# First branch's gates ahead of the second branch's operands, LayerNorm and RG-LRU in one pool, step sizes beside attention, PSUM handed over by bank

## The chip, the core and the metric

The kernel runs on one NeuronCore of a Trainium2 chip. The metric is the device time of one launch in microseconds (us), the median of several runs. All matrix products are float32 values split in two parts of a narrower float32 format, so that one product is three matmuls (high by high, high by low, low by high).

## What is computed

One layer of a streaming encoder for 1024 prompt frames and 64 sample frames (T = 1088 columns), 1024 channels, four branches:

```python
h = rms_norm(x, p['norm_pre']); proj = h @ p['w_in']          # 80 chunks of 128 columns, and 8 columns ssd_dt
u_a = rg_lru(causal_dwconv(lru_x)) * silu(lru_g)              # a_t = exp(-8 r softplus(-lam)), h_t = a_t h_{t-1} + ...
u_b = rms_norm(ssd_scan(...) * silu(ssd_z))                   # dt = softplus(ssd_dt + dt_bias), chunks of frames
u_c = silu(layer_norm(causal_dwconv(glu))) * silu(cf_g)
u_d = stick_breaking(q, k, v) * silu(sb_g)
mixed = sum over b of sigmoid(merge_b) * (u_b @ w_down[b])
y = x + rms_norm(mixed @ w_out)
```

## The kernel before, in words

Activations lie channel-major in `hh` and `hl`, 128 x 8 x 1088 each, the high and low part of the normalised input. A chunk of the input projection is 24 matmuls for each of three column pieces (384, 384, 320). The program runs in stages that TensorE works through in written order (L193: its order is the program's; the other engines' queues and the queue of SyncE, which issues all transfers, are ordered by a planner that goes by program order, with head starts such as W_PRIO for weight splits and C_PRIO for evacuations).

1. **Head**: normalise and transpose the input.
2. **Attention**: 68 units of scores, stick-breaking and output; between two units `feed.step` puts pieces of the other projections (L532: a quota that reaches 18 pieces per group of 17 units; in the last of the four groups 15 pieces are there). Constants for the SSD branch (`wdr`, `wd2`, `dtb_t`, `a_t`, `dsk`) stand behind this stage in the program.
3. **Spill stage** (L574 to L660): four chunks of the gate of branch C, in 12 pieces, each evacuated by ScalarE into `t` and stored; between them the sums and differences of the quarters of `hh` and `hl` (`g11`, `g12`, `g22`, `g21`: eight sums of 128 x 1088 on GpSimd at L601, the differences on VectorE) and their splits into `Th` and `Tl`; the product for the step sizes (L619, 48 matmuls), its transposes (L625), the softplus (`spd`), `adt`, and the two cumulative products at L641.
4. **Pair stage** (L663 to L1073): 20 pairs of chunks (gates of A, z of B, merge gates), each by a seven-product scheme (`ORDER`); after each of the 140 products a generator `chains()` is advanced by one step. It runs LayerNorm of branch C (`layer_norm`, 27 steps), RG-LRU (`lru`, a pool of its own on the right side of SBUF, three steps of waiting, then eight rounds of four steps) and SSD (`ssd`, three steps of waiting behind its first loads, then nine chunks). PSUM is a new pool here, `bank` x6 and `pg2` x2.
5. **Down stage** (L1079 on): for branch order 3, 0, 2, 1 and eight blocks of 128 rows each, a product into PSUM (`pj3` x6), multiplied by the gate `sga` (loaded by L1118, sigmoid at L1119) into `m`. `Operand` (L1082) loads a branch's `u` over dead parts of `hh` and `hl`. PSUM is a third pool.

A LayerNorm quarter q: `load`, mean product (L772), square, fold, three steps, variance product (L779), `lnr`, scale, SiLU, gate, split into `lnh` and `lnl`, stores (L793, L794), three steps. An RG-LRU round (c, j): load of `lg_t`, products for the two gates in two halves with a step between them, next round's `load`, Exp and Tanh (L852, L853), Sqrt, scan (L860), times `lg_t`, split into `uah` (which takes the slot of `ga`) and `ual` (which takes the slot of `lg_t`), stores, three steps.

A pool that is opened with `reuse_waits="tile"` makes each tile wait for what lay at its own addresses; without it, every tile of the new pool waits for the whole old pool.

Of the kernel before, what the change touches and what calls it, by code (L numbers as in the profile page):

```python
# [8 lines left out]
FT = mybir.dt.float32  # L9
# [36 lines left out]
def encoder_step(ctx, tc, x, prm, win, wdt, wdn, wout, lwa, lwx, ckT, cv_, ssd0, npre, npost, dtb, alog, dskip,  # L46
# [10 lines left out]
    ps = ps1.enter_context(tc.tile_pool(name="ps", bufs=1, space=PSUM))  # L57
# [452 lines left out]

    feed.add(cf_sig(0), cf_glu(0), k_chunk(0), q_chunk(0), g_chunk(0))
# [9 lines left out]
    for m, u in enumerate(units):  # L521
        c, k = divmod(m, NU)
        if k == 0:
            if c < 3:
                feed.add(cf_sig(c + 1), v_chunk(c + 1) if c else extra.pop(0), extra.pop(0), g_chunk(c + 1), cf_glu(c + 1), extra.pop(0))
            else:
                feed.add(*extra)
            fed = 0
# [3 lines left out]
        want = min(18, 18 * (k + 1) // (NU - 1))  # L532
# [19 lines left out]
        else:  # L552
# [3 lines left out]
            u.output(None)  # L556
    p1.close()
    p2.close()

    wdr = const.tile([128, 8, 8], FT, name="wdr")  # L560
    dma(wdr, wdt)
    wd2 = const.tile([128, 8, 16], FR, name="wd2")
    S.activation(wd2[:, :, 0:8], wdr, AF.Copy)
    V.tensor_sub(wd2[:, :, 8:16], wdr, wd2[:, :, 0:8].bitcast(FT))
    dtb_t = const.tile([128, 8], FT, name="dtb_t")
    dma(dtb_t, ap(dtb, 0, [[0, 128], [1, 8]]))
    a_t = const.tile([128, 8], FT, name="a_t")
    dma(a_t, ap(alog, 0, [[0, 128], [1, 8]]))
    S.activation(a_t, a_t, AF.Exp)
    dsk = const.tile([128, 4], FT, name="dsk")  # L570
    for h in range(2):
        dma(dsk[h * 64:h * 64 + 64, :], ap(dskip, h, [[0, 64], [2, 4]]))
# [15 lines left out]
    feed.add(*(spill(C_CG + c, cg_d[:, c]) for c in range(4)))  # L588
    feed.step(1)
# [6 lines left out]
    for k in (0, 2):  # L596
        g11, g12, g22 = (tmp.tile([128, 2, HT], FT, name=f"g{n}") for n in (11, 12, 22))
        g21 = tmp.tile([128, 2, HT], FT, name="g21", bufs=2)
        for g, kk, t in ((g11, k, tlo), (g12, k, thi), (g22, k + 4, thi), (g21, k + 4, tlo)):
            ks = slice(kk, kk + 2)  # L600
            G.tensor_tensor(g, hh[:, ks, t].bitcast(FT), hl[:, ks, t].bitcast(FT), op=OP.add)  # L601
# [8 lines left out]
        t4.append((kd, g21))  # L610
    feed.step(2)


    dtr = tmp.tile([16, T], FT, name="dtr")
    for i, (t0, n) in enumerate(SPL):
        p = pg()
        for k in range(8):
            for q, hx in enumerate((hh, hl)):
                PE.matmul(p[:16, :n], wd2[:, k, :], hx[:, k, t0:t0 + n], start=k == 0 and q == 0, stop=k == 7 and q == 1)  # L619
        S.activation(dtr[:, t0:t0 + n], p[:16, :n], AF.Copy)  # L620
    feed.step(3)
    pd = pg()
    for i in range(9):
        r = 128 if i < 8 else 64
        PE.transpose(pd[:r, i * 16:i * 16 + 16], dtr[:, i * 128:i * 128 + r], ident[:16, :16])  # L625
    pd3 = pd[:, :144].rearrange("p (i c) -> p i c", c=16)
    zb = tmp.tile([128, 9, 8], FT, name="zb", bufs=1)
    V.memset(zb, 0.0)
    for r, i0, i1 in ((128, 0, 8), (64, 8, 9)):
        V.tensor_tensor(zb[:r, i0:i1], pd3[:r, i0:i1, 0:8], dtb_t[:r, None, :].to_broadcast([r, i1 - i0, 8]), op=OP.add)  # L630
        V.tensor_tensor(zb[:r, i0:i1], pd3[:r, i0:i1, 8:16], zb[:r, i0:i1], op=OP.add)
    dt = dq.tile([128, 9, 8], FT, name="dt", bufs=1)
    V.tensor_copy(dt, softplus(tmp, zb, [9, 8], "spd"))
    adt = dq.tile([128, 9, 8], FT, name="adt", bufs=1)
    V.scalar_tensor_tensor(adt, dt, -1.0, a_t[:, None, :].to_broadcast([128, 9, 8]), op0=OP.mult, op1=OP.mult)
    V.memset(adt[64:128, 8, :], 0.0)
    feed.step(4)
    pa = pg()
    a2 = adt.rearrange("p i c -> p (i c)")
    PE.matmul(pa[:, 0:72], tri_le, a2, start=True, stop=True)  # L640
    PE.matmul(pa[:, 72:144], ones, a2, start=True, stop=True)  # L641
    acs = dq.tile([128, 2, 72], FT, name="acs", bufs=1)
    V.tensor_copy(acs, pa[:, :144].rearrange("p (a b) -> p a b", a=2))
    dtd = dq.tile([128, 9, 8], FT, name="dtd", bufs=1)
    d2 = dtd.rearrange("p i c -> p (i c)")
    V.tensor_sub(d2, acs[:, 1], acs[:, 0])
    S.activation(d2, d2, AF.Exp)
    S.activation(acs, acs, AF.Exp)
    eacs, etot = acs[:, 0], acs[:, 1]
    ah = dq.tile([128, 9, 8], FR, name="adh", bufs=1)  # L650
    al = dq.tile([128, 9, 8], FR, name="adl", bufs=1)
    split(ah, al, adt)
    V.tensor_tensor(dtd, dtd, dt, op=OP.mult)
# [9 lines left out]
    ps = ps2.enter_context(tc.tile_pool(name="ps2", bufs=1, space=PSUM))  # L663
# [84 lines left out]

    def layer_norm():
        lnp = ExitStack()  # L750
        ln = lnp.enter_context(tc.tile_pool(name="ln", bufs=1, side="right", reuse_waits="tile"))

# [13 lines left out]
        for q in range(4):  # L766
# [27 lines left out]
            dma(ul_d[2][:, :, t], gw.bitcast(FT))  # L794
            yield from wait(3)
        lnp.close()


    def lru():
        p4 = ExitStack()  # L800
        lp = p4.enter_context(tc.tile_pool(name="lru", bufs=1, side="right", reuse_waits="tile"))
        nl = lp.tile([128, 4], FT, name="nl")
        V.tensor_scalar(nl, P("lam", 0, 4), -1.0, None, op0=OP.mult)
        sp = softplus(lp, nl, [4], "spl")
        lm8 = lp.tile([128, 4], FT, name="lm8")
        lp4 = lp.tile([128, 4], FT, name="lp4")
        V.tensor_scalar(lm8, sp, -8.0, None, op0=OP.mult)
        V.tensor_scalar(lp4, sp, 4.0, None, op0=OP.mult)
        hfin = lp.tile([128, 2, 4], FT, name="hfin")
        raws = [lp.tile([128, 128], FT, name=f"bd{e}") for e in "ax"]  # L810
        for r_ in raws:
            G.memset(r_, 0.0)

        def load(c, j):
            t = slice(j * HT, j * HT + HT)
            if j == 0:
                self.bd = []
                for r_, src, e in zip(raws, (lwa, lwx), "ax"):
# [3 lines left out]
                    self.bd.append([lp.tile([128, 128], FR, name=f"bd{e}{f}") for f in "hl"])  # L822
                    split(*self.bd[-1], r_)
            xc = lp.tile([128, HT], FT, name="xl", bufs=2)
            dma(xc, xl_d[:, c, t])
            xh, xl = (lp.tile([128, HT], FR, name=f"xg{f}") for f in range(2))
            split(xh, xl, xc)
            return xc, xh, xl

        class self:  # L830
            pass
        todo = [(c, j) for c in range(4) for j in range(2)]
        nxt = load(0, 0)
        yield from wait(3)
        for m, (c, j) in enumerate(todo):
            t = slice(j * HT, j * HT + HT)
            xc, xh, xl = nxt
            g = lp.tile([128, HT], FT, name="lg_t")
# [3 lines left out]
            for t0 in (0, QT):  # L842
# [4 lines left out]
                if t0 == 0:  # L847
                    yield
# [410 lines left out]
```

## Time and profile before

| what | value |
|---|---|
| median of 3 runs | 1485.22 us (1483.89 to 1486.68) |
| profiled execution, its own time | 1485.71 us |
| span of its instructions | 1483.3 us |
| TensorE matmul busy | 1413.3 us (95%) |
| VectorE, ScalarE, GpSimd busy | 1067.1, 673.0, 263.0 us |
| mean granted TensorE clock | 0.986 |

A page of the profile gives busy times by engine, the span in 40 slices, and the costliest groups of instructions. Views of the trace give the waits by engine, single instructions in order of time with the idle time before them in brackets and what ended it, and sums over chosen stretches. TensorE's clock has two levels, 1.2 and 2.4 GHz, and the granted clock 0.50 and 1.00 of a stretch are these two.

### The profile page before, as it was taken

The page shows a single profiled execution, that of the slowest core. Times are in us where ns is not written, and L with a number is a line of the kernel's source. Part 1 is how long each engine was busy: PE and PEld are TensorE (multiplying, and loading weights), DVE is VectorE, ACT ScalarE, POOL GpSimd, SP SyncE. Part 2 cuts the span into 40 slices and gives each one's busy share as a digit, 9 for nine tenths or more (in the row PEclk, how much of TensorE's full clock was granted, in tenths as well). Part 3 has the DMA queues.
Part 4 walks back from the last instruction along what each step waited for, and adds up shares of the span by engine and source line. Part 5 has one row for each costly group of instructions (what it writes and reads, how often), then busy time and mean ns, then how long its engine had stood idle before and what let it go on. Part 6 is the DMA issues. An engine that isn't in the chain of part 4 may idle for free.

```text
span 1483.3 us, 25336 instructions
## 1 busy us (share of the span) xinstructions
PE 1413.3 (95%) x9857; PEld 1352.0 (91%) x9857; DVE 1067.1 (72%) x1628; ACT 673.0 (45%) x1225; POOL 263.0 (18%) x245
## 2 busy tenths in 40 slices
PE   6999999999999999899979989999999889999997
PEld 6899999999999998799979989999999789999885
DVE  6289889779879987847967775787877335669433
ACT  6324544544454365345769762443444242234211
POOL 0002221230221224613213231221211000000000
PEclk9999999999999999999989999999999989999999
DMA  6231212213212233134635444434343985643322
GB/s 210 75 87 54 82 47 83 87 55 95 84 56 79 66 102 107 41 125 142 212 135 175 152 138 139 131 108 154 120 133 96 329 333 170 244 155 109 105 86 71
DMA packets 113335, 184.43 MB, mean 124 GB/s; under 512 B 22080, under 2 KB 70080, under 8 KB 112704
## 3 DMA queue, kind: packets, MB, share of 16 engines
q1 hardware_dynamic: 113216, 182.82, 37.8%
q8 instruction: 77, 1.26, 0.4%
q14 instruction: 42, 0.34, 0.1%
HBM read 118.00 MB, written 60.59 MB: 120 GB/s over the span
## 4 chain that ended last, share of the span: by engine, by line
PE 40%; DVE 7%; ACT 4%; DMA 4%; issue 2%; SPq 0%; DVEq 0%; ACTq 0%
PE bank L721 16%; PE pj L109 7%; PE pj L110 7%; PE pj L111 7%; DVE w_lo L229 2%; DMA uh<-uoh 1%; DMA uh<-uah 1%; ACT w_hi L228 1%; DMA sga<-mgs 1%; PE pg L912 1%; DVE r L728 1%; PE pg L965 1%; ACT L852 1%; DVE lnx L787 0%; DVE yz L1005 0%
## 5 line engine op out<-in xcount | busy, mean ns | idle before, releaser
L110 PE MATMUL pj<-hl,w_hi 128*128 128x384 f32 (+4 forms) x1184 | 384.8, 325 | 1.6 <-DVE hl L225 1.6
L109 PE MATMUL pj<-hh,w_hi 128*128 128x384 f32 (+4 forms) x1088 | 354.7, 326 | 8.2 <-ACT t L584 5.5
L111 PE MATMUL pj<-hh,w_lo 128*128 128x384 f32 (+4 forms) x1088 | 352.3, 324 | 0.0
L110 PEld LDWEIGHTS pj<-hl,w_hi 128*128 128x128 f32 x1184 | 225.5, 190 | 3.5 <-DVE hl L225 2.5
L109 PEld LDWEIGHTS pj<-hh,w_hi 128*128 128x128 f32 x1088 | 206.5, 190 | 11.0 <-ACT t L584 5.6
L111 PEld LDWEIGHTS pj<-hh,w_lo 128*128 128x128 f32 x1088 | 206.2, 190 | 0.2
L721 PE MATMUL bank<-hh,w_hi 128*128 128x272 f32 x640 | 189.6, 296 | 1.8 <-ACT t L584 1.8
L721 PE MATMUL bank<-hh,w_lo 128*128 128x272 f32 x640 | 185.1, 289 | 0.0
L721 PE MATMUL bank<-hl,w_hi 128*128 128x272 f32 x640 | 185.1, 289 | 0.0
L243 DVE SCALAR_TENSOR_TENSOR cvo<-cbuf,p_t,cvo 128x1118 f32<-128x1118 f32 x120 | 165.5, 1380 | 1.8
L721 PE MATMUL bank<-Th,w_hi 128*128 128x272 f32 x480 | 143.1, 298 | 0.5 <-ACT r L725 0.5
L721 PE MATMUL bank<-Th,w_lo 128*128 128x272 f32 x480 | 139.8, 291 | 0.0
L721 PE MATMUL bank<-Tl,w_hi 128*128 128x272 f32 x480 | 139.6, 291 | 0.0
L721 PEld LDWEIGHTS bank<-hh,w_hi 128*128 128x128 f32 x640 | 121.4, 190 | 3.5 <-ACT t L584 2.0
L721 PEld LDWEIGHTS bank<-hl,w_hi 128*128 128x128 f32 x640 | 121.3, 189 | 0.6
L721 PEld LDWEIGHTS bank<-hh,w_lo 128*128 128x128 f32 x640 | 121.0, 189 | 0.0
L460 POOL TENSOR_SCALAR_AFFINE_SELECT fb<-fb 128x128 f32<-128x128 f32 (+1 forms) x72 | 38.6, 536 | 453.1 <-ACT fb L455 332.1
L463 DVE TENSOR_TENSOR_SCAN fb<-fb,ones 128x128 f32<-128x128 f32 (+8 forms) x68 | 90.0, 1324 | 27.5 <-POOL fb L460 27.4
L725 ACT ACTIVATE r<-bank 128x272 f32<-128x272 f32 x160 | 62.0, 391 | 91.1 <-PE bank L721 90.8
L102 DVE TENSOR_TENSOR w_lo<-w_raw,w_hi 128x1024 fp32r<-128x1024 f32 x56 | 70.9, 1266 | 44.4 <-ACT w_hi L101 43.9
L721 PEld LDWEIGHTS bank<-Th,w_hi 128*128 128x128 f32 x480 | 92.1, 192 | 2.6 <-issue 1.2
L101 ACT ACTIVATE w_hi<-w_raw 128x1024 fp32r<-128x1024 f32 x56 | 59.4, 1060 | 77.2 <-PE pj L110 69.1
(345 smaller groups left out, 2978.6 us busy)
## 6 DMA issues: line engine op xcount, KB each, us to landing
w_raw<-in_win_dram SPq DMA_DIRECT2D x80, 512.0 KB, 4.0
mgs<-r SPq DMA_DIRECT2D x64, 272.0 KB, 2.1
sga<-mgs SPq DMA_DIRECT2D x32, 544.0 KB, 4.2
w_raw<-in_wdn_dram SPq DMA_DIRECT2D x16, 512.0 KB, 4.6
xt<-in_x_dram SPq DMA_DIRECT2D x8, 512.0 KB, 9.4
xbc<-xc SPq DMA_DIRECT2D x8, 512.0 KB, 2.7
xb<-xbc SPq DMA_DIRECT2D x8, 512.0 KB, 5.6
w_raw<-in_wout_dram SPq DMA_DIRECT2D x8, 512.0 KB, 4.1
```

Of the source, the lines that this page charges most:

```text
L101: S.activation(hi, r3, AF.Copy)
L102: V.tensor_sub(lo, r3, hi.bitcast(FT))
L109: PE.matmul(out, ah, bh, start=first, stop=False)
L110: PE.matmul(out, ah, bl, start=False, stop=False)
L111: PE.matmul(out, al, bh, start=False, stop=last)
L228: S.activation(hi, src, AF.Copy)
L229: V.tensor_sub(lo, src, hi.bitcast(FT))
L243: V.scalar_tensor_tensor(out[:, :n], b[:, i:i + n], w[:, i:i + 1], out[:, :n], op0=OP.mult, op1=OP.add)
L460: G.affine_select(t_[s, 1024 - w:1024], t_[s, 1024 - w:1024], pattern=[[-1, w]], compare_op=OP.is_gt, fill=fill, base=0, channel_multiplier=1)
L463: V.tensor_tensor_scan(F[:, rev], F[:, rev], ones[:, 0:1].to_broadcast([128, n]), 1.0, OP.mult, OP.mult)
L721: PE.matmul(p, a_[:, k], b_[:, k, s], start=new and k == 0 and z == 0, stop=k == 3 and z == 2, skip_group_check=True)
L725: S.activation(R[to][:, s], p, self.last if j == 4 else AF.Copy)
```

## The change

It does eight things: all three PSUM pools are opened with `reuse_waits="tile"`; the constants of the SSD branch stand ahead of attention; the step-size product and its transposes become a generator fed in the last group of attention units, whose quota ends at 17; the softplus takes `lam` of RG-LRU along (76 columns) and stands at the head of the spill stage; the eight sums are VectorE's; the cumulative products stand between the two halves of the sums. LayerNorm's pool stays open for RG-LRU, whose tiles take LayerNorm's slots (`xg` that of `lnh`, `eg` that of `lng`, `rx` that of `lnx`, `uah`/`ual` that of `lns`, every second `xl` that of `lnq`); its first loads stand in LayerNorm's third and fourth quarter and its three waiting steps are gone; SSD waits five steps instead of three. In the down stage the eight gates of the first branch are loaded ahead of the second branch's operand, and their pool lies ahead of that of `m`.

```diff
-    ps = ps1.enter_context(tc.tile_pool(name="ps", bufs=1, space=PSUM))
+    ps = ps1.enter_context(tc.tile_pool(name="ps", bufs=1, space=PSUM, reuse_waits="tile"))
...
+    def step_sizes():
+        dtr = cp.tile([128, T], FT, name="dtr", tag="sb", bufs=1)
+        dts.append(dtr)
+        yield
+        for t0, n in SPL:
+            p = pg()
+            for k in range(8):
+                for q, hx in enumerate((hh, hl)):
+                    PE.matmul(p[:16, :n], wd2[:, k, :], hx[:, k, t0:t0 + n], start=k == 0 and q == 0,
+                              stop=k == 7 and q == 1)
+            S.activation(dtr[:16, t0:t0 + n], p[:16, :n], AF.Copy)
+            yield True
+        pd = dts[0] = pg()
...
-                feed.add(*extra)
+                feed.add(*extra, step_sizes())
...
-        want = min(18, 18 * (k + 1) // (NU - 1))
+        want = min(18 - (c == 3), (18 - (c == 3)) * (k + 1) // (NU - 1))
...
+    V.tensor_scalar(zl[:, 72:76], P("lam", 0, 4), -1.0, None, op0=OP.mult)
+    sp = softplus(tmp, zl, [76], "spd")
...
-            G.tensor_tensor(g, hh[:, ks, t].bitcast(FT), hl[:, ks, t].bitcast(FT), op=OP.add)
+            V.tensor_tensor(g, hh[:, ks, t].bitcast(FT), hl[:, ks, t].bitcast(FT), op=OP.add)
...
+        if k == 0:
+            feed.step(2)
+            pa = pg()
+            a2 = adt.rearrange("p i c -> p (i c)")
+            PE.matmul(pa[:, 0:72], tri_le, a2, start=True, stop=True)
...
-    ps = ps2.enter_context(tc.tile_pool(name="ps2", bufs=1, space=PSUM))
+    ps = ps2.enter_context(tc.tile_pool(name="ps2", bufs=1, space=PSUM, reuse_waits="tile"))
...
             if q < 3:
                 nxt = load(q + 1)
+            if q == 2:
+                lru.fetch(0, 0)
...
+            if q == 3:
+                lru.prepare(0, 0)
             yield from wait(3)
-        lnp.close()
...
+        def fetch(self, c, j):
             if j == 0:
...
+            xc = self.xc[c, j] = ln.tile([128, HT], FT, name="xl", tag=("xl", "lnq")[j])
+            dma(xc, xl_d[:, c, j * HT:j * HT + HT])
+
+        def prepare(self, c, j):
+            self.xg = ln.tile([128, 2, HT], FR, name="xg", tag="lnh")
+            split(self.xg[:, 0], self.xg[:, 1], self.xc[c, j])
+
+        def run(self):
...
+                eg = ln.tile([128, 2, HT], FT, name="eg", tag="lng")
+                ga, g = eg[:, 0], eg[:, 1]
+                dma(g, lg_d[:, c, t])
+                rx = ln.tile([128, 2, HT], FT, name="rx", tag="lnx", bufs=2)
+                gr, gx = rx[:, 0], rx[:, 1]
...
+                uh = ln.tile([128, HT], FR, name="uah", tag="lns", bufs=2)
+                ul = ln.tile([128, HT], FR, name="ual", tag="lns", bufs=2)
...
-        yield from wait(3)
+        yield from wait(5)
...
-    ps = ctx.enter_context(tc.tile_pool(name="ps3", bufs=1, space=PSUM))
+    ps = ctx.enter_context(tc.tile_pool(name="ps3", bufs=1, space=PSUM, reuse_waits="tile"))
...
-    us.append(Operand(order[1], [t_[:, k, thi] for t_ in (hh, hl) for k in (k0, k1)]))
-    mp = ctx.enter_context(tc.tile_pool(name="mp", bufs=1, reuse_waits="tile"))
-    mt = [mp.tile([128, T], FT, name=f"m{d}") for d in range(8)]
...
-    gates = [load_gate(order[0], d) for d in range(8)]
+    gates = [load_gate(order[0], d) for d in range(4)]
+    mp = ctx.enter_context(tc.tile_pool(name="mp", bufs=1, reuse_waits="tile"))
+    mt = [mp.tile([128, T], FT, name=f"m{d}") for d in range(8)]
+    gates += [load_gate(order[0], d) for d in range(4, 8)]
+    us.append(Operand(order[1], [t_[:, k, thi] for t_ in (hh, hl) for k in (k0, k1)]))
```

## Rows read from the trace of the kernel before

**Rows 1.** Waits of TensorE: instruction <- released by: us in total, times, longest us.
```profile
PE pj L109 <- DVE m L1150: 9.1, 1, 9.1
...
PE pg L109 <- ACT xg L228: 8.1, 1, 8.1
PE pj L109 <- ACT t L584: 5.5, 1, 5.5
PE pg L912 <- DVE lt L902: 4.5, 1, 4.5
...
PE pg L109 <- ACT gr L846: 2.7, 1, 2.7
PE pg L475 <- DVE beta L464: 2.3, 1, 2.3
...
PE bank L721 <- ACT t L584: 1.8, 1, 1.8
...
PE pj L109 <- ACT rs__12675 L1002: 1.4, 1, 1.4
```
**Rows 2.** Sums over stretches behind five waits: stretch, length, busy by engine, PEclk, DMA.
```profile
621.90:626.00 4.10, 4.10 (x13) 4.10 (x14) 4.10 (x4) 2.86 (x4) 0.00 (x0) 0.50 0.13 48
...
757.40:762.50 5.10, 4.93 (x20) 4.62 (x21) 0.70 (x1) 2.31 (x4) 0.00 (x0) 0.50 0.08 21
...
851.20:854.70 3.50, 3.50 (x17) 3.50 (x17) 3.47 (x9) 2.60 (x7) 1.00 (x1) 0.51 0.40 159
...
889.30:895.60 6.30, 6.30 (x22) 5.27 (x23) 3.15 (x6) 1.59 (x3) 0.00 (x0) 0.50 1.05 269
...
1190.40:1196.00 5.60, 5.60 (x25) 5.60 (x26) 2.10 (x6) 4.62 (x5) 0.00 (x0) 0.50 1.03 411
```
**Rows 3.** Sums over a stretch, of L619 alone: length, PE busy, PEld busy, PEclk, DMA.
```profile
595.00:604.00 9.00, 8.06 (x48) 4.53 (x48) 1.00 0.00 0
```
**Rows 4.** Spill stage: sum of L601 on POOL, three instructions, sum of tile spd.
```profile
583.87:648.20 64.33, 24.17 (x8) 0.95 0.23 76
...
605.93 3.63 DVE L607 TENSOR_TENSOR g<-g,g 128x1088 f32<-128x1088 f32 x1
...
622.73 1.28 DVE L607 TENSOR_TENSOR g<-g,g 128x1088 f32<-128x1088 f32 x1
...
620.32 1.11 ACT L228 ACTIVATE Th<-g 128x1088 fp32r<-128x1088 f32 x1 [9.30 <-DVE g L603]
...
627.50:634.50 7.00, 4.11 (x17) 0.26 (x1) 1.00 0.38 126
```
**Rows 5.** LayerNorm's last quarter to RG-LRU: instructions, one piece of the chain, landing of `lnh`.
```profile
730.48 0.72 PE L779 MATMUL pg<-lns,ones 128*128 128x272 f32 x2 [0.28 <-DVE lns L756]
...
731.20 15.07 PE bank L721 x120
...
743.77 1.11 ACT L228 ACTIVATE lnh<-lnx 128x1088 fp32r<-128x1088 f32 x1
...
DMA to landing us min/median/max: 3.3/3.6/4.3
...
756.68 0.66 ACT L228 ACTIVATE xg<-xl 128x544 fp32r<-128x544 f32 x1 [1.02 <-DMA xl<-xls]
```
**Rows 6.** RG-LRU: ScalarE's wait ahead of Exp, and a group in SyncE's queue.
```profile
842.75 1.28 ACT L852 ACT_TABLE_LOAD   x1 [2.81 <-DMA uh<-uah]
...
843.73 8.33 SPq L738 DMA_DIRECT2D mgs<-r  x3
```
**Rows 7.** Start of the down stage: SyncE's queue, ScalarE's wait, landing of the two weights.
```profile
1178.27 18.75 SPq L1118 DMA_DIRECT2D sga<-mgs  x10
1197.07 1.40 SPq L96 DMA_DIRECT2D w_raw<-in_wdn_dram  x1
...
1188.73 1.11 ACT L1119 ACTIVATE sga<-sga 128x1088 f32<-128x1088 f32 x1 [12.96 <-DMA sga<-mgs]
...
DMA to landing us min/median/max: 5.2/5.2/5.2
```

More of the change, by code (lines that the diff above doesn't have):

```diff
@@ L509, in output @@
             dma(ul_d[3][:, c, i * 128:i * 128 + m], ul[:, :m].bitcast(FT))
+    wdr = const.tile([128, 8, 8], FT, name="wdr")
+    dma(wdr, wdt)
+    wd2 = const.tile([128, 8, 16], FR, name="wd2")
+    S.activation(wd2[:, :, 0:8], wdr, AF.Copy)
+    V.tensor_sub(wd2[:, :, 8:16], wdr, wd2[:, :, 0:8].bitcast(FT))
+    dtb_t = const.tile([128, 8], FT, name="dtb_t")
+    dma(dtb_t, ap(dtb, 0, [[0, 128], [1, 8]]))
+    a_t = const.tile([128, 8], FT, name="a_t")
+    dma(a_t, ap(alog, 0, [[0, 128], [1, 8]]))
+    S.activation(a_t, a_t, AF.Exp)
+    dsk = const.tile([128, 4], FT, name="dsk")
+    for h in range(2):
+        dma(dsk[h * 64:h * 64 + 64, :], ap(dskip, h, [[0, 64], [2, 4]]))
+    dts = []
+    def step_sizes():
[11 more added lines that the diff above has]
+        pd = dts[0] = pg()
+        for i in range(9):
+            r = 128 if i < 8 else 64
+            PE.transpose(pd[:r, i * 16:i * 16 + 16], dtr[:16, i * 128:i * 128 + r], ident[:16, :16])
+        yield True
     feed.add(cf_sig(0), cf_glu(0), k_chunk(0), q_chunk(0), g_chunk(0))
@@ L556, in encoder_step @@
             u.output(None)
+    pd = dts[0]
     p1.close()
     p2.close()
[L560 to L572, printed above, removed]
     a1 = ExitStack()
@@ L610, in encoder_step @@
         t4.append((kd, g21))
-    feed.step(2)
[L614 to L625, printed above, removed]
@@ L634, in encoder_step @@
[L634 to L643, printed above, removed]
@@ L794, in layer_norm, with __init__ @@
             dma(ul_d[2][:, :, t], gw.bitcast(FT))
+            if q == 3:
+                lru.prepare(0, 0)
             yield from wait(3)
-        lnp.close()
[L799 to L815, printed above, removed]
+    class Lru:
+        def __init__(self):
+            self.raws = [ln.tile([128, 128], FT, name=f"bd{e}") for e in "ax"]
+            for r_ in self.raws:
+                V.memset(r_, 0.0)
+            self.hfin = ln.tile([128, 2, 4], FT, name="hfin")
+            self.xc = {}
+        def fetch(self, c, j):
             if j == 0:
-                self.bd = []
-                for r_, src, e in zip(raws, (lwa, lwx), "ax"):
+                for r_, src in zip(self.raws, (lwa, lwx)):
                     for h in range(2):
@@ L877, in ssd @@
+    lru = Lru()
     def ssd():
@@ L1042, in chains @@
         yield from layer_norm()
-        yield from lru()
+        yield from lru.run()
         yield from ssd()
```

141 lines of the change are left out of this document (70 added, 71 removed).

## The prediction, made before the change was run

> **What bounds the kernel now.** TensorE is busy 1413.3 of 1483.3 us, so nothing that another engine saves counts unless TensorE waited for it. I therefore read first the waits of TensorE alone [rows 1]. The eight rows there are places, not habits: each comes once. A first wait of 9.1 us for `st` is the head, which the change leaves alone; it isn't shown. What is left is 9.1 us at the start of the down stage, 8.1 at the first RG-LRU product, 5.5 in the spill stage, 4.5 at the start of SSD, 2.7 in the middle of RG-LRU, 2.3 at the end of attention, and 1.8 and 1.4 where one PSUM pool follows another. The second view is the granted clock just behind five of these waits [rows 2]: it stands at 0.50, the 1.2 GHz level, for 4.1, 5.1, 3.5, 6.3 and 5.6 us in which TensorE works. At half speed half of each stretch is lost: 2.0, 2.5, 1.7, 3.1 and 2.8 us. So a wait costs more than its row says, and one that goes gives the slow stretch back too. Behind the waits of 2.3, 1.8 and 1.4 us the clock stayed up.
>
> **End of attention.** The 48 step-size matmuls take 8.06 us of TensorE wherever they stand [rows 3]; moving them gains only what idle time they fill. In the last group of units the 15 pieces run out two units before the end, and the last big unit's transposes wait 2.3 us for `beta` [rows 1]. With the quota of 17 two thirds of the product, some 5 us, fall just there, between those scores and those transposes, so the 2.3 us are covered: gain 2.3. The third piece and the transposes come behind; their evacuation by ScalarE is short, and I take nothing for it. The constants moved ahead of attention have five small loads, an Exp and a split; nothing of them is waited for in the trace, and I take 0. If SyncE should issue them ahead of a weight block, a block would be late by their issue time, at most some 2 us.
>
> **Spill stage.** Eight sums on GpSimd take 24.17 us, 3.0 each, and the same VectorE subtraction takes 3.63 us beside them and 1.28 us once GpSimd is idle [rows 4]. ScalarE's split into `Th` then waits 9.30 us for VectorE [rows 4], the evacuation of `t` is queued behind that split on ScalarE, and TensorE runs out of PSUM: 5.5 us and 2.0 of slow clock. With the sums on VectorE each operation costs 1.28: 22 of them for sums, differences and splits make 28 us, and the softplus with its waits another 7.0 [rows 4], 35 us in all against about 47 us in which TensorE works through the 12 pieces (the 64.33 us of the stretch [rows 4] less 5.5, 2.0, 8.06 and some 1.5 of transposes and cumulative products). So VectorE has room, and no ScalarE split can wait for more than about three operations, 4 us, while three PSUM tiles of 4 us each are in flight. Gain 7.5. The change adds one wait: the cumulative product now stands behind three pieces, and in TensorE's queue all later pieces stand behind it. The three pieces take about 11.8 us; `adt` needs 7.0. Cover 4.8 us, so 0; if VectorE comes late from attention by more than that, 1 to 3 us. The evacuation of the last piece no longer holds the first `bank`: gain 1.8, or 0 if the planner keeps the pool's wait.
>
> **Start of RG-LRU.** Here I differ from what the edit suggests. In the kernel before the product stands six steps behind the variance product of LayerNorm's last quarter: that one stands at 730.48 to 731.20, a step takes 3.0 us (120 matmuls in 15.07 us are five of them), so TensorE runs dry at some 749.3 [rows 5]. Without the three waiting steps TensorE comes to the same product three steps sooner, at 740.2 of this timeline. Is `xg` ready by then? The loads are, they stand a quarter ahead. But `xg` takes the slot of `lnh`, and `lnh` of the last quarter is written at 743.77 to 744.88 at the end of a chain from 730.48 on that runs through VectorE and ScalarE and that the change leaves alone; its store must land first, 3.3 to 4.3 us later; the split of `xg` takes 0.66 [rows 5]. That makes 748.9, and a wait of 8.7 us in place of 8.1. The removed loads and the four-column softplus are thus not missed: what ended last moves from RG-LRU's own loads to LayerNorm's store. I take a loss of 0.6 and the same slow stretch. The bounds are a loss of 2 (the loads of the third quarter put four small splits into queues that are near full) and a gain of 10.6, the whole wait with its 2.5 us, if the planner runs the last quarter's chain far sooner.
>
> **Middle of RG-LRU and start of SSD.** In a round of RG-LRU Exp writes `ga`, whose slot `uah` of the round before still held until its store landed: ScalarE stood 2.81 us for that in the worst round and held the sigmoids behind it [rows 6], and so TensorE waited 2.7 us. Now Exp waits for VectorE's product with `lg_t` alone, which ends before the split and the store. Gain 2.7 and 1.7 of clock, bound 0 if another slot takes over. SSD's first product is reached two steps, 6.0 us, later than before behind RG-LRU's last, and the wait was 4.5 [rows 1]: gain 4.5 and 3.1. Cover is 1.5 us, more if RG-LRU's last round is shortened as said. The generator as a whole is one step shorter (27 + 32 + 79 for 27 + 35 + 77), so SSD's last `norm` comes one step sooner.
>
> **Start of the down stage.** Gate 0 was issued at 1178.27 behind the second operand's four loads, and ScalarE waited 12.96 us for it while the six `pj3` tiles filled [rows 7]. Now the gates stand ahead, over the tiles `T6` and `T5`, which the last pair leaves after its fourth product of seven. Gate 0 has some 10 us more and is needed 9 us after TensorE's arrival: gain 9.1 and 2.8. The second operand is first needed 8 blocks of 6.0 us (48 matmuls at the pace of [rows 5]) later; it lands long before. The 1.4 us of pool change [rows 1] go with the earlier `norm`.
>
> **The sum.** 2.3 + 7.5 + 1.8 - 0.6 + 4.4 + 7.6 + 13.3 = 36.3 us. The profiled execution took 1485.7 us (2.4 outside its span) and the median of the runs is 1485.2, so the forecast is **1449 us**. Its own range, by the bounds above, is 1444 to 1457.
>
> **Rivals.** *A, the RG-LRU start closes as well.* The same sum with a gain of 10.6 in place of a loss of 0.6 gives 1438. For it: ScalarE and VectorE idle a little in that chain. Against it: the chain is serial, 14.4 us plus store, against three steps of 3.0.
>
> *B, the weights of the down stage come late.* TensorE now arrives at the third pair of blocks four blocks, 24 us, after 1170.5, at 1194.6. Its weights were issued at 1197.07, behind gates of the next branch, and landed 5.2 us later [rows 7], 7.7 us too late if they keep that time, and with a slow stretch of 2.8 and the 2 to 3 us of their splits some 13 us: 1462. The Trainium skill bears on this: "DMA: Bandwidth & Descriptors", section "Two DMAs through the same engine are not ordered", says that within one queue descriptors start in order. By that rule a block of weights issued behind eight gates and an operand waits until they have started, and the sum would be that of this rival; by the landing time of 5.2 us in the row the queue had by then run short. No row shows where the weights stand after the change, so this keeps a chance.
>
> *C, slower: the ring of RG-LRU.* `ga` and the loaded gate now share the tile `eg`. If Exp had to wait for the load into the other half, each round would hang on SyncE's queue, where one group of stores took 8.33 us [rows 6]. TensorE's work in a round is four steps and the products, and it reaches the next round's products without waiting for anything else; from 4.5 us a round on, times eight, the 36 us are gone, and with 6 a round it is 1497. Against it: the load goes out some 10 us before Exp.
>
> *D, no change:* the planner's new order moves the waits elsewhere, 1484.
>
> **Chances.** Forecast 0.55, A 0.22, B 0.17, C 0.04, D 0.02. The range 1437 to 1464 takes in the forecast, A and B. A measurement of this kernel can tell about 0.2%, 3 us, from no change. Faster 0.94, within 0.2% 0.02, slower 0.04.
>
> **What would show it.** In the changed kernel's waits of TensorE: no row for `t`, `lt`, `m` and `rs`; a row for `xg` of 8 to 9 us at some 16 us earlier in the span than before, with ScalarE idle for the store of `lnh`; the clock at 0.50 behind that row alone, besides head and tail. The same VectorE subtraction at 1.28 us throughout the spill stage. The prediction is wrong if the `xg` row is gone (then A), or if a row for weights or for `pj` stands in the down stage (then B).

## Result: 1503.9 us, slower by 1.2%

The changed kernel takes 1503.91 us, median of 4 runs (1503.63 to 1504.18), against 1485.94 us of four runs of the kernel before (1483.89 to 1486.68). The ratio is 1.0122 with a 95% interval of 1.0110 to 1.0134. Forecast were 1449 us and a faster kernel: wrong in sign. The waits of TensorE after the change, head and small ones left out (released by: us in total, times, longest):

```profile
PE pg L655 <- DVE adt L628: 24.0, 1, 24.0
PE pj L109 <- ACT w_hi L101: 18.5, 1, 18.5
PE pg L109 <- ACT xg L228: 10.7, 1, 10.7
...
PE pg L109 <- ACT rx L859: 5.3, 4, 3.5
...
PE bank L738 <- ACT r L742: 2.2, 3, 1.1
```

Set beside [rows 1]: the rows for `m` (9.1), `t` (5.5 and 1.8), `lt` (4.5), `beta` at L475 (2.3) and `rs` (1.4) are gone, as forecast. Two large ones are new, `adt` and the down weights `w_hi`. `xg` has grown from 8.1 to 10.7, and the waits for `r` from 0.5 to 2.2. In the middle of RG-LRU 5.3 for `rx` stand in place of 4.5: `rx` is the pair of tiles `gr` and `gx` under a new name, and before it was 2.7 for `gr` and

```profile
PE pg L109 <- ACT gx L846: 1.8, 2, 0.9
```

The same in three stages: up to the first product of the first pair, from there to the first product of the down stage, and the rest. Columns: stretch, length, busy of PE, PEld, VectorE, ScalarE, GpSimd, PEclk, share of DMA, GB/s. Before:

```profile
0.00:649.92 649.92, 620.71 (x4178) 593.07 (x4178) 520.69 (x636) 301.91 (x582) 144.33 (x164) 0.99 0.27 83
649.92:1171.93 522.01, 498.11 (x3904) 486.18 (x3904) 383.90 (x658) 282.84 (x509) 118.70 (x81) 0.98 0.46 150
1171.93:1483.30 311.37, 294.54 (x1776) 272.79 (x1776) 162.47 (x336) 88.26 (x134) 0.00 (x0) 0.98 0.49 169
```

After:

```profile
0.00:664.40 664.40, 620.70 (x4177) 593.46 (x4178) 517.54 (x647) 301.13 (x579) 120.12 (x156) 0.98 0.26 81
664.40:1181.79 517.39, 495.84 (x3906) 483.43 (x3905) 373.07 (x647) 285.32 (x511) 114.56 (x79) 0.99 0.47 151
1181.79:1502.30 320.51, 293.87 (x1778) 272.04 (x1776) 161.88 (x330) 88.47 (x135) 0.00 (x0) 0.96 0.48 165
```

The stages changed by +14.5, -4.6 and +9.1 us, together +19.0, the difference of the spans. The prediction's terms for them are -11.6 (2.3 + 7.5 + 1.8), -12.8 (+0.6, -4.4, -7.6 and the -1.4 of pool change) and -11.9 (9.1 + 2.8). So it missed by 26.1, 8.2 and 21.0 us. TensorE does the same work: its busy time differs by 2.9 us in all, and what grew is its idle time.

**The first place, `adt`.** VectorE in the spill stage after the change, in order of time (start, duration, instruction, in brackets idle time before it):

```profile
597.68 0.22 DVE L253 SCALAR_TENSOR_TENSOR spd<-zb 128x76 f32<-128x76 f32 x1
...
613.78 0.22 DVE L261 SCALAR_TENSOR_TENSOR spd<-spd,spd 128x76 f32<-128x76 f32 x1
613.93 1.28 DVE L641 TENSOR_TENSOR g<-hh,hl 128x1088 f32<-128x1088 f32 x1
615.13 0.22 DVE L261 SCALAR_TENSOR_TENSOR spd<-spd,spd 128x76 f32<-128x76 f32 x1
615.28 1.28 DVE L641 TENSOR_TENSOR g<-hh,hl 128x1088 f32<-128x1088 f32 x1
616.48 0.22 DVE L261 SCALAR_TENSOR_TENSOR spd<-spd,spd 128x76 f32<-128x76 f32 x1
...
626.31 0.07 DVE L628 MEMSET adt<- 64x8 f32 x1
```

Here lies the change's largest loss. Each step of the softplus depends on the one before it, and behind each stands one large sum, difference or split of 1.28 us. A step thus takes 1.35 us, and the chain runs from 597.7 to 626.4. In the kernel before seven of these steps ran one behind the other, at 0.26 us each:

```profile
631.53 1.84 DVE L261 SCALAR_TENSOR_TENSOR spd<-spd,spd 128x72 f32<-128x72 f32 x7
```

TensorE stands at the cumulative product from 602.5 on, with all nine pieces that are left queued behind it.

**The second place, the down weights.** SyncE's queue after the change (start, duration, issue):

```profile
1192.96 0.70 SPq L1106 DMA_DIRECT2D hl<-ul  x1
1193.77 5.47 SPq L1130 DMA_DIRECT2D sga<-mgs  x1
1199.34 0.65 SPq L96 DMA_DIRECT2D w_raw<-in_wdn_dram  x1
```

This load of weights is the second block, which TensorE needs at 1194.05. In the kernel before it was issued ahead of operand and gates:

```profile
1164.78 0.39 SPq L96 DMA_DIRECT2D w_raw<-in_wdn_dram  x1
```

Now it stands behind eight gates, the operand's four loads and one gate of the next branch. The view of L96 from 1190 to 1205 us has the landing of this load and of the next block's, 12.1 us and 13.3 us after the issue, against 5.2 in [rows 7]:

```profile
DMA to landing us min/median/max: 12.1/12.7/13.3
```

ScalarE's split of the block starts as it lands (1199.34 and 12.1 make 1211.44), just behind the sigmoid of that same next gate:

```profile
1210.24 1.11 ACT L1131 ACTIVATE sga<-sga 128x1088 f32<-128x1088 f32 x1 [12.30 <-DMA sga<-mgs]
1211.44 1.06 ACT L101 ACTIVATE w_hi<-w_raw 128x1024 fp32r<-128x1024 f32 x1
```

The 16 DMA engines were busy 80% or more all through 1176 to 1215 (13.92 MB). The queue rule from the Trainium skill that the prediction set beside rival B ("DMA: Bandwidth & Descriptors", section "Two DMAs through the same engine are not ordered": descriptors of one queue start in order) agrees with these rows as far as they go: the operand's last load landed 15.8 us after its issue at 1192.96, the next gate 16.4 us after 1193.77, and the block, issued behind these 13 loads, after them all. When its descriptors started no row shows.

**The clock.** Behind the three large waits TensorE worked at half clock (PEclk 0.50) for 4.0, 3.9 and 4.5 us, half of which is lost, some 6 us. Some 3.4 us at 0.50 more stand behind a wait of 2.27 us for `beta` in the middle of attention (last section) and about 3 behind the 3.5 us for `rx`. The stretches behind the three:

```profile
626.42:630.43 4.01, 4.00 (x14) 4.00 (x15) 2.01 (x5) 2.01 (x4) 0.00 (x0) 0.50 0.00 0
765.53:770.37 4.84, 3.93 (x16) 3.63 (x17) 1.44 (x1) 2.22 (x3) 0.86 (x1) 0.50 0.27 79
...
1212.55:1217.52 4.97, 4.53 (x18) 4.21 (x19) 2.88 (x3) 2.17 (x2) 0.00 (x0) 0.50 1.00 419
```

### The profile page after: what moved, and what is told of

Same layout as the page of the kernel before. It is cut to its first block, busy times and chain, and to the rows that moved or that the text cites. A ratio compares the mean times of both kernels' runs of the same rounds, so it can differ in the third digit from the quotient of the medians.

```text
span 1502.3 us, 25343 instructions
## 1 busy us (share of the span) xinstructions
PE 1410.4 (94%) x9857; PEld 1348.9 (90%) x9857; DVE 1052.5 (70%) x1622; ACT 674.9 (45%) x1224; POOL 234.7 (16%) x235
## 4 chain that ended last, share of the span: by engine, by line
PE 51%; DVE 6%; ACT 4%; DMA 3%; issue 2%; SPq 0%; DVEq 0%; ACTq 0%
PE bank L738 20%; PE pj L111 8%; PE pj L109 8%; PE pj L110 8%; DMA w_raw<-in_wdn_dram 1%; DVE w_lo L229 1%; PE pg L980 1%; DVE rx L873 1%; PE pg L493 1%; PE pg L536 1%; PE pg L927 1%; DMA lng<-cg 1%; ACT w_hi L228 1%; PE pg L936 0%; PE pg L475 0%
## 5 line engine op out<-in xcount | busy, mean ns | idle before, releaser
L109 PE MATMUL pj<-hh,w_hi 128*128 128x384 f32 (+4 forms) x1088 | 355.4, 327 | 19.9 <-ACT w_hi L101 18.5
```

The lines of the kernel that those rows point to most:

```text
L109: PE.matmul(out, ah, bh, start=first, stop=False)
```

## Experiments

All are edits of the changed kernel; "before" stands for runs of the kernel before on the same chip. The theory was: `adt` is late because VectorE's order alternates its chain with large operations (T, made sharper as T2), the weights because gates and operand stand ahead of them in one queue (Q), and the first RG-LRU product by the slot that it shares with `lnh` (X). The rivals were VectorE's total work (R1, R3), the product's place alone (R2), a slot of `w_raw` that comes free late (S), and ScalarE's order (Y).

| run | us, median | ratio to before, 95% interval |
|---|---|---|
| the change | 1503.91 | 1.0122 (1.0110 to 1.0134) |
| e1 product late | 1478.16 | 0.9946 (0.9929 to 0.9963) |
| e2 sums on GpSimd | 1512.86 | 1.0180 (1.0161 to 1.0198) |
| e3 weights first | 1495.69 | 1.0067 (1.0051 to 1.0082) |
| e4 operand later | 1491.00 | 1.0032 (1.0020 to 1.0043) |
| e5 short chain | 1496.64 | 1.0073 (1.0056 to 1.0090) |
| e6 xg in another slot | 1496.27 | 1.0072 (1.0057 to 1.0087) |
| e7 quota 18 | 1506.34 | 1.0138 (1.0123 to 1.0153) |
| e8 three fixes | 1456.91 | 0.9807 (0.9792 to 0.9822) |
| e9 gates' call back | 1502.93 | 1.0106 (1.0092 to 1.0120) |
| e10 SSD waits three | 1508.07 | 1.0146 (1.0130 to 1.0161) |
| e11 sigmoids first | 1471.57 | 0.9897 (0.9883 to 0.9912) |
| e12 down part undone | 1494.63 | 1.0049 (1.0034 to 1.0064) |
| e13 pool back | 1495.85 | 1.0061 (1.0044 to 1.0078) |
| e14 pool back, fixes | 1455.35 | 0.9788 (0.9774 to 0.9803) |

### What makes `adt` late: e1, e2, e5

**e1, the product later.**

```diff
         if k == 0:
             feed.step(2)
-            pa = pg()
...
-    feed.step(2)
+    feed.step(7)
+    pa = pg()
```

> The changed kernel with one thing moved: the cumulative product stands behind ten pieces of the spill stage (steps 1, 2 and 7) instead of three; the order of VectorE stays about as it is. Theory T (the chain of some twenty small softplus operations is dealt out between big ones on a VectorE that is never idle, one big operation of 1.28 us for each, so adt ends 29 us after the chain's first operation wherever the product stands): adt still ends 35 to 37 us after the stage's first piece, TensorE gets there after some 40, the wait of 24.0 us falls to 0 to 1 and the 2 us of half clock behind it go: 1476 to 1479. Rival R1 (VectorE has too much work in the stage, the wait only moves): another wait of 10 us or more stands in the stage, for t or for the operands T6, T5, T7 of the first pair, and the time is 1488 or more.

1478.16 us; the product waits for nothing, and no other wait has taken its place. Up to the first pair 637.63 us pass with a clock of 1.00, against 664.40 in the change and 649.92 before:

```profile
0.00:637.63 637.63, 618.27 (x4177) 591.34 (x4178) 516.73 (x646) 299.96 (x579) 124.50 (x156) 1.00 0.27 84
```

`adt` itself is as late as in the change, its last piece at 626.81 and its chain from 596.71 on: 30.1 us. So R1 falls, VectorE has room; only the place at which TensorE asks for `adt` was wrong.

**e2, the sums back on GpSimd.**

```diff
-            V.tensor_tensor(g, hh[:, ks, t].bitcast(FT), hl[:, ks, t].bitcast(FT), op=OP.add)
+            G.tensor_tensor(g, hh[:, ks, t].bitcast(FT), hl[:, ks, t].bitcast(FT), op=OP.add)
```

> The changed kernel with the eight sums back on GpSimd, the product where the change put it. Theory T (the delay of adt is the number of big operations that lie ready on VectorE beside the chain): the sums come from GpSimd at 3 us each, so fewer differences and splits lie ready while the chain runs; adt ends earlier and the wait is 8 to 18 us, 1488 to 1498. Rival R2 (the product simply stands too early, its own chain takes this long, whoever makes the sums): the wait stays within 2 us of 24.0 and the time at 1502 to 1506.

1512.86 us and a wait of 33.6: both expectations missed. VectorE in that run:

```profile
600.49 3.62 DVE L643 TENSOR_TENSOR g<-g,g 128x1088 f32<-128x1088 f32 x1 [6.44 <-POOL g L641]
604.21 3.39 DVE L644 TENSOR_TENSOR g<-g,g 128x1088 f32<-128x1088 f32 x1
607.52 2.48 DVE L255 TENSOR_SCALAR spd<-spd 128x76 f32<-128x76 f32 x1
```

The chain's third step, L255, could have run at 598.4, when ScalarE's Exp was done. It stands behind L643 and L644, which wait for GpSimd and then run at 3.6 and 3.4 us beside it, as L607 did in [rows 4]. So my theory was wrong in one point: it is not how many large operations lie ready, but which stand ahead in VectorE's fixed order. The Trainium skill says so of this engine ("PSUM — Partial Sum Buffer", section "Engine vs sequencer instructions": the queues of ScalarE, VectorE and GpSimd are strictly first in, first out), and these rows agree.

**e5, a shorter chain.**

```diff
-        for m in (15, 13, 11, 9, 7, 5, 3):
+        for m in (3,):
```

> The changed kernel with one step of the softplus polynomial instead of seven (the other six terms are left out); everything else as in the change. It tells what the wait of 24.0 us for adt is made of. Theory T2 (VectorE runs its instructions in one fixed order, in which the chain and the large operations alternate, so each small step of 0.22 us costs also the large one of 1.28 us that stands behind it): six steps less bring adt 6 x 1.35 = 8 us earlier, the wait is 15 to 17 us, the time 1494 to 1498. Rival R3 (the wait is VectorE's total work up to adt, whatever the order): six steps save 6 x 0.15 = 0.9 us, the wait is 22 to 24 us, the time 1501 to 1505.

```profile
PE pg L655 <- DVE adt L628: 15.8, 1, 15.8
```

1496.64 us, within T2's range. Six steps less took 8.1 us from the wait (23.95 to 15.84), 1.35 each, where their own work is 0.15 each. R3 falls: the wait is the alternation, not the sum of VectorE's work.

### The down stage: e3, e4, e9, e12, e13

**e3, the second block ahead of the gates.**

```diff
+    nw2 = weights(wdn[order[0], 1])
     gates = [load_gate(order[0], d) for d in range(4)]
...
-                    nwd = weights(...)
+                    nwd = nw2 if bi == 0 and d == 1 else weights(...)
```

> The changed kernel with the second block of down weights issued and split ahead of the gates instead of behind gates and operand. Theory Q (the block waits its turn in the one queue of loads behind 8.8 MB of gates and operand): the wait of 18.5 us for w_hi goes with some 2 us of half clock; the third block is the next in danger, since it still stands behind three gates of the next branch, and may cost 3 to 10 us: 1486 to 1496. Rival S (the block is late because its slot w_raw comes free late): the wait stays at 15 us or more, 1500 to 1506.

```profile
PE pj L109 <- ACT w_hi L101: 10.3, 1, 10.3
```

1495.69 us. The second block is in time; the 10.3 us are the third block's, which comes behind gates, operand and three gates of the next branch. **e4, the operand behind the third block:**

```diff
-    us.append(Operand(order[1], ...))
...
                     nwd = weights(...)
+                if bi == 0 and d == 3 and i == 0:
+                    us.append(Operand(order[1], ...))
```

> The changed kernel with the four loads of the second operand moved behind the third block of weights, into the loop; the gates stay ahead. Theory Q: the second block is now issued behind the eight gates and one gate of the next branch alone; these end at about 1198 in the changed kernel's trace, so the block lands at about 1200 and TensorE waits some 6 to 9 us instead of 18.5: 1491 to 1495. Rival S (slot of w_raw): 18.5 stays, 1500 to 1506.

1491.00 us, with 5.6 us for `w_hi`: the second block waits for the eight gates and one of the next branch. In both runs rival S falls, since the slot of `w_raw` was free early enough.

**e9, the order of the calls undone:** the operand's line stands ahead of the gates again.

> The changed kernel with one part undone: the second operand's four loads stand ahead of the eight gates again, as before the change. It prices the part that was to save 9.1 us. Theory Q: gate 0 comes late again, TensorE waits some 9 us for m behind the first blocks and loses 2 to 3 us of clock, but the second block of weights finds its place in the queue earlier, as before, and the wait of 18.5 us with its 2.5 us goes: 1492 to 1499, so that the part as made costs 5 to 12 us. Rival S (the second block is late for another reason than the gates' place): the wait for w_hi stays at 10 us or more, 1503 to 1515.

1502.93 us and 17.7 us for `w_hi`: Q misses, and by the wait it is the rival S of this run, "another reason". The block is issued at 1200.06, as late as in the change. What the undo left in place is where the gates lie: their pool is still opened ahead of that of `m`, over `T6` and `T5`. e12 and e13 take this apart.

**e12, order and place undone:**

```diff
+    us.append(Operand(order[1], ...))
+    mp = ctx.enter_context(tc.tile_pool(name="mp", bufs=1, reuse_waits="tile"))
+    mt = [mp.tile([128, T], FT, name=f"m{d}") for d in range(8)]
     sgp = ctx.enter_context(tc.tile_pool(name="sgp", bufs=1, reuse_waits="tile"))
...
-    gates = [load_gate(order[0], d) for d in range(4)]
-    mp = ...
-    mt = ...
-    gates += [load_gate(order[0], d) for d in range(4, 8)]
-    us.append(Operand(order[1], ...))
+    gates = [load_gate(order[0], d) for d in range(8)]
```

> The changed kernel with the whole down part undone: operand ahead of the gates, and the pool of m ahead of the pool of the gates, so that the gates lie where they lay before. Theory Pl (the place decides: over T6 and T5 the gates are ready as early as the slot of w_raw, and SyncE's order puts them and the operand ahead of the block): the block is issued ahead of the gates, the wait of 18.5 us for w_hi goes, the old one of 9 us for m comes back with its 3 us of clock: 1492 to 1498. Rival O (something outside the part, such as PSUM handed over by bank or SSD's new end): a wait of 15 us or more for w_hi stays, 1502 or more.

The second block in SyncE's queue:

```profile
1175.49 0.38 SPq L96 DMA_DIRECT2D w_raw<-in_wdn_dram  x1
```

and TensorE's wait in the down stage:

```profile
PE pj L109 <- DVE m L1165: 11.1, 1, 11.1
```

1494.63 us. The block is issued 24 us earlier, its wait is gone, and the old one for `m` is back. The down part as the change made it therefore costs 9.3 us (1503.91 less 1494.63) where it was to gain 11.9. Of the 9.3, 7.5 lie in the down stage itself, which takes 313.0 us here and 320.5 in the change.

**e13, the place alone undone:** as e12, with the operand behind the gates.

> The changed kernel with the place of the gates alone undone: the gates are still called ahead of the operand, but the pool of m lies ahead of theirs. Theory Pl: the second block is issued ahead of the gates; the gates come at the end of the last pair, ahead of most of the operand, and TensorE waits 3 to 6 us for m instead of 18.5 for w_hi; the third block, behind gates and operand, may cost up to 10 us: 1488 to 1498. Rival (the order of the calls decides, not the place): 16 to 19 us for w_hi stay, 1501 to 1505.

The same two views:

```profile
1174.49 0.38 SPq L96 DMA_DIRECT2D w_raw<-in_wdn_dram  x1
```

```profile
PE pj L109 <- DVE m L1165: 3.5, 1, 3.5
PE pj L109 <- ACT w_hi L101: 3.5, 1, 3.5
```

1495.85 us. With the gates called first but lying behind `m` the block comes in time too, so the place decides: with either order of the calls the block is issued at 1199 to 1200 where the gates lie over `T6` and `T5` (the change, e9), and at 1174 to 1176 where they lie behind `m` (e13, e12). Why is argued, not shown: over `T6` and `T5` the gates may be loaded as soon as those two are dead, before the last pair ends, and SyncE's order then has them ahead of the block, which is called later. The third block, behind gates and operand, is 3.5 us late. The profiled execution is the fastest of e13's four (1492.9), with 311.5 us in the down stage against 313.0 in e12; why the median is no better than e12's stays open.

### RG-LRU, SSD, attention: e6, e10, e7, e11

**e6, `xg` in the slots `lns`.**

```diff
-            self.xg = ln.tile([128, 2, HT], FR, name="xg", tag="lnh")
+            self.xg = [ln.tile([128, HT], FR, name=f"xg{f}", tag="lns", bufs=2) for f in "hl"]
...
-                uh = ln.tile([128, HT], FR, name="uah", tag="lns", bufs=2)
-                ul = ln.tile([128, HT], FR, name="ual", tag="lns", bufs=2)
+                ua = ln.tile([128, 2, HT], FR, name="ua", tag="lnh")
+                uh, ul = ua[:, 0], ua[:, 1]
```

> The changed kernel with two slots exchanged: xg takes the two tiles lns, which are free after the variance product, and uah with ual takes lnh. Theory X (the first RG-LRU product waits for the store of lnh of LayerNorm's last quarter, through the shared slot): the split of xg stands right behind its load, the wait of 10.7 us falls to 0 to 2, its half clock of some 3 us goes too: 1489 to 1494. Rival Y (the real end is the late chain of the last quarter on ScalarE, in whose order the first sigmoids stand behind the split into lnh): xg comes early, but TensorE then waits 4 to 10 us for a PSUM tile or for rx: 1494 to 1502.

1496.27 us. In the change ScalarE came to the split so:

```profile
764.81 0.66 ACT L228 ACTIVATE xg<-xl 128x544 fp32r<-128x544 f32 x1 [3.44 <-DMA uh<-lnh]
```

In e6 TensorE's waits have no row for `xg`, but more for `rx`:

```profile
PE pg L109 <- ACT rx L859: 8.6, 8, 3.5
```

and the stretch behind the first two of these, in the columns of the stages above, is

```profile
761.85:768.72 6.87, 5.96 (x24) 5.64 (x25) 4.15 (x4) 3.32 (x7) 4.27 (x3) 0.50 0.51 167
```

The wait for `xg` is gone, as X says; its slot was the reason. But 2.0 and 0.9 us for `rx` came in its place, part of the 8.6, and behind them TensorE works 6.0 us at half clock, more than the 3.9 in the change. So 7.6 us are saved and not 10 or more, and the time lies in Y's range, not in X's: X named the slot rightly, and Y that TensorE would then wait for `rx`.

**e10, SSD waits three steps.**

```diff
-        yield from wait(5)
+        yield from wait(3)
```

> The changed kernel with one part undone: SSD waits three steps again instead of five. It tests the step of the prediction that held, the wait of 4.5 us for lt at SSD's start with 3.1 us of clock. If those two steps bought the gain, the wait comes back and the time is 1507 to 1512. Rival Z (the wait went because RG-LRU ends otherwise): no wait for lt, 1502 to 1505.

```profile
PE pg L927 <- DVE lt L917: 2.1, 1, 2.1
```

1508.07 us, 4.2 more than the change. The step holds; its price is 4.2 and not the 7.6 of the sum, since the wait that comes back is 2.1 long and not 4.5.

**e7, the quota at 18.**

```diff
-        want = min(18 - (c == 3), (18 - (c == 3)) * (k + 1) // (NU - 1))
+        want = min(18, 18 * (k + 1) // (NU - 1))
```

> The changed kernel with the quota of the last group of attention units at 18 instead of 17. Theory U (with 17 one unit in the middle of the group gets one piece where it had two, and its scores then wait 2.3 us for beta with 1.7 us of half clock behind it): this wait goes, no wait comes back at the end of the group: 1499 to 1501. Rival V (the wait comes from the constants or the other order of VectorE, not from the quota): 2.3 us stay and the time is 1502.5 to 1505; or it moves to the end of the group, where it was before the change.

1506.34 us, and the wait of 2.3 us in the middle stays: U falls. That wait is no part of the change. The kernel before has it too, in order of time on TensorE:

```profile
521.47 0.50 PE L442 MATMUL pz<-kh,qs 128*128 128x512 f32 x1 [2.23 <-ACT beta L456]
```

Waits of 0.9 and 0.4 us came back at the end of attention. The time lies outside both ranges, and V's reason (constants, VectorE's order) falls too, since the wait is older than they are. Whether the quota of 17 gains 2 us can't be told; the intervals of e7 and the change overlap.

**e8, three fixes.** The edits of e1, e3, e4 and e6 together, and in the down stage the first four gates of the next branch called later:

```diff
             if bi < 3:
-                gates[d] = load_gate(order[bi + 1], d)
+                if bi or d > 3:
+                    gates[d] = load_gate(order[bi + 1], d)
+                if not bi and d in (4, 6):
+                    for e in (d - 4, d - 3):
+                        gates[e] = load_gate(order[1], e)
```

> The changed kernel with three things: the cumulative product behind ten pieces (as before in this study), xg in the slots lns, and in the down stage the second block of weights ahead of the gates, the second operand behind the third block, and the first four gates of the next branch two or four blocks later. If the three waits are what the change loses by and no other stands behind them, they add: 1503.9 - 25.7 (measured for the product) - 18.5 - 3 (down stage) - 10.7 - 3 (xg) = 1443, and 1440 to 1450 with small rests. Rival: one of the three waits is replaced by the next in line (a fourth block of weights behind gates, a PSUM tile in RG-LRU), 1452 to 1465.

1456.91 us, in the rival's range: the three waits are gone, but their savings don't add. Of the 14 us that lack, 6.1 lack in RG-LRU as e6 alone had shown (7.6 for 13.7), and 8.4 in the down stage, which takes 307.4 us and so gains 13.1 on the change's 320.5 in place of 21.5: two blocks of weights come late by 1 to 2 us each, with a stretch of half clock behind each.

**e11, sigmoids ahead.** e8 with one edit:

```diff
-                        S.activation(dst[:, t0:t0 + QT], p, AF.Sigmoid, bias=bias)
+                        with tc.high_priority(offset=H_PRIO):
+                            S.activation(dst[:, t0:t0 + QT], p, AF.Sigmoid, bias=bias)
```

> The kernel with the three fixes (1456.9) and one more: ScalarE's sigmoids of RG-LRU stand ahead of the splits of uah and lnh in its order. Theory W (the rests in RG-LRU of 2.0, 1.3, 1.1 and 3.5 us, with 10.2 us of half clock behind them of which some 5 are worked, come from the place of the sigmoids behind those splits): they go for the most part, 1447 to 1452. Rival: the chain of Exp, scan and products is what RG-LRU takes in a round, whatever the order: waits of the same sum for xg or rx, 1455 to 1458.

1471.57 us, 14.7 slower than e8; W falls, and the rival's 1455 to 1458 is missed as well. Waits of TensorE between 735 and 880 us, where e8 has 7.1 us for `rx` and 1.7 for `r`:

```profile
PE pg L109 <- ACT rx L860: 7.9, 4, 2.7
PE pg L110 <- DVE hfin L875: 4.4, 2, 3.0
PE pg L110 <- DVE xgl L229: 2.8, 2, 2.0
```

The sigmoids of the next round now stand between Exp and Tanh of the round before; that round's scan ends later, and the lower half of `xg` stands behind the scan on VectorE (`hfin` is its last value). Another order has only moved the wait. That the chain of a round is what bounds RG-LRU is argued from this, not shown.

**e14, the place undone and the fixes.** e8 with e13's pool order in place of e3's edit.

> The kernel with the three fixes (1456.9), its down stage made in another way: the pool of m ahead of the gates' (instead of the second block called ahead of the gates), the second operand behind the third block and the first four gates of the next branch later, as there. By theory Pl blocks two and three stand ahead of all gates; a wait of 4 to 6 us for m with 2 of clock stands against small waits for w_hi of 4.3 us with 3 of clock in that kernel: 1453 to 1460, about the same. By the rival of e13 the second block is late by 15 us or more: 1468 or more.

1455.35 us, in the range of theory Pl, 2.1% faster than the kernel before (0.9788, 0.9774 to 0.9803) and the lowest median here, though the intervals of e14 and e8 overlap.

```profile
0.00:637.77 637.77, 618.41 (x4177) 591.34 (x4178) 516.68 (x646) 299.98 (x579) 124.11 (x156) 1.00 0.27 84
637.77:1148.85 511.08, 497.60 (x3906) 484.72 (x3905) 374.03 (x647) 284.02 (x511) 114.64 (x79) 0.99 0.48 153
1148.85:1453.00 304.15, 292.19 (x1778) 270.25 (x1776) 161.38 (x330) 88.86 (x135) 0.00 (x0) 0.99 0.50 173
```

Set beside the stages of before: 12.2, 10.9 and 7.2 us less. That is 30.3 of the 36.3 us forecast, once the two new waits are gone; but e6's slots and the later gates of the next branch, which the change did not have, are part of it.

## Why the prediction was wrong, point by point

- **End of attention, spill stage, PSUM: right, 11.6 forecast, 12.3 measured** (649.92 to 637.63 us in e1, where nothing else waits). No wait for `t`, no wait at the handover, VectorE's large operations at 1.28 us: as said, but for one sum of 2.24 us and one difference of 2.37 in the change, both while GpSimd worked.
- **The cumulative product: the step that failed most.** The text says "`adt` needs 7.0. Cover 4.8 us, so 0". The term mis-sized is the 7.0; it measured 29 us, and cost 24.0 of wait and 2.0 of clock, where the first stage missed by 26.1. The 7.0 came from a stretch of before in which all but one of VectorE's large operations were done: besides the chain's own 4.11 us [rows 4] there was one weight split of 1.21, and VectorE was busy 6.13 of the 7.00. The change puts one large operation behind each step. I had added up VectorE's work (35 of 47 us; in e1 it is busy 38.4 of 47.0, from 590.6 to 637.6) and not asked what stands between two steps of a chain. The range of 1 to 3 us was set by the same wrong picture. e1 and e5 show it.
- **Start of RG-LRU: the mechanism right, the size right in most traces.** `xg` did wait for the store of `lnh`, with ScalarE idle 3.44 us for it: 10.7 us for the 8.7 forecast, so a loss of 2.6 and not 0.6, beyond the bound of 2. But the excess belongs to single executions. In this one `lnh` came later, behind the load of `lng`, for which VectorE waited 3.19 us. Ten of the runs have this part unchanged: where they wait 2.2 to 3.1 us for `lng` (e1, e2, e4, e10), `xg` costs 9.7 to 10.6, and in the six without that wait (e3, e5, e7, e9, e12, e13) it costs just what was forecast:

```profile
PE pg L109 <- ACT xg L228: 8.7, 1, 8.7
```

  Why `lng` lands late in some executions no row shows. Rival A is refuted by the row; e6 shows that the slot was the reason.
- **Middle of RG-LRU: wrong.** Exp no longer waits for a store, as said, yet TensorE's waits there rose from 4.5 to 5.3 us instead of falling by 2.7. I took the slot for the bound. In the longest of them, 3.5 us up to 876.48, what the trace shows ahead of the sigmoid is ScalarE's order: its split into `uah` waits for VectorE's last product, as in every round, and the sigmoids that empty PSUM stand behind that split. ScalarE's waits in the change from 740 to 900 us:

```profile
ACT uah L228 <- DVE rx L878: 16.1, 8, 2.8
```

  That this order is the bound is argued: e11 moved the sigmoids ahead of the split and was slower. What would shorten the round stays open.
- **Start of SSD: right, too large.** Forecast 7.6, measured 4.2 (e10), where the wait that came back was 2.1 us long and not 4.5. The `rs` wait of 1.4 went as said.
- **Down stage: wrong, rival B in a worse form.** The gates did come in time and the 9.1 us for `m` went. But the text moved only the gates and asked of the weights no more than B did, at the third pair of blocks, 24 us into the stage, and for 13 us. It was the second block, 12.3 us into the stage (1194.05, from 1181.79 on), for 18.5 us and 2.3 of clock, a term that the sum did not have. What the working left out was whether a load that stood ahead of the gates stays ahead when the gates become ready sooner. The queue rule set beside B gave the right direction: one rival with 0.17 was too little for it.
- **Chances.** Rival C, the only slower one, was refuted: no round of RG-LRU waits for the load into `eg`. The kernel is slower by two mechanisms that had a sentence each in the working (a cover of 4.8 us, a block of weights) and no place in the chances for slower.

## What to carry to other kernels

A chain of small dependent operations takes its own time only where its engine is otherwise idle; move other work onto that engine and each step costs the operation that is put behind it, so multiply the steps by that operation before giving the chain a consumer with little cover. When a load is allowed to start earlier, by its place in memory as much as by its place in the program, list what it overtakes in the queue and when each of these is needed. And before taking a row's length for a cost, look at what stood between its steps there and what will stand there now.

## What the hardware showed that I had not expected

- The same 512 KB of weights landed 5.2 us after its issue with three gates still under way [rows 7] and 12.1 to 13.3 us behind gates and operand, with the DMA engines busy throughout.
- With seven loads under way, three gates and the operand's four, one issue on SyncE took 5.47 us where its neighbours took 0.65 to 0.70, and no row of that queue names a wait that long; what held it is open.
- One and the same short wait can cost the clock or not. The wait of 2.2 to 2.3 us for `beta` near 521 us stands in all sixteen traces; in eight (before, e1, e7, e8, e11 to e14) the clock stays at 1.00 behind it, and in the other eight, the change among them, it falls to 0.50 for about 3 us (in the change to 524.6, from 521.2 on), also where the program up to there is the same (the change and e12). So some 1.7 us of the change's first stage belong to that execution.
- Two short waits of 2.0 and 0.9 us, 1.0 us of work apart, had half clock behind them: 0.50 for the 6.9 us from the end of the first on (e6); a single one of 1.9 us in e14, up to 1160.03, stands in a stretch at full clock:

```profile
1158.00:1166.00 8.00, 6.05 (x48) 5.97 (x48) 4.50 (x10) 6.88 (x7) 0.00 (x0) 1.00 1.02 412
```
